# Another order for a hand-written passage, two sums on VectorE, other banks and a later sample product in the first ConvFFN slices

## The chip, the core and the metric

The kernel runs on one core of a Trainium2 chip. The core has four engines that work side by side, each through its own ordered stream of instructions: TensorE (PE) for matmuls, VectorE (DVE), ScalarE (ACT) and GpSimd (POOL) for everything elementwise. A fifth, SyncE (SP), issues most DMAs. An instruction waits at the head of its engine's stream until the semaphores it needs are set; what is queued behind it waits too. Matmul results land in PSUM banks, everything else lies in SBUF. The metric is the device time of one execution in microseconds (us); less is better.

## What is computed

One inference step of a hybrid decoder layer, for 1024 prompt rows and 64 sample rows (8 sequences of 8), with a model width of 1024. The part that matters here is the end of the attention half and the beginning of the feed-forward half:

```python
def rmsnorm(x, g):
    xf = x.astype(jnp.float32)
    y = xf * lax.rsqrt(jnp.mean(xf * xf, axis=-1, keepdims=True) + EPS)
    return (y * g.astype(jnp.float32)).astype(x.dtype)

def conv_ffn(n, prev, lw):
    a = n @ lw['ffn_w_gate']
    c = n @ lw['ffn_w_up']
    T = a.shape[1]
    full = jnp.concatenate([prev.astype(a.dtype), a], axis=1)
    w = lw['ffn_conv_w']
    conv = lw['ffn_conv_b'] + sum(w[j] * full[:, j:j + T] for j in range(CONV_W))
    y = (jax.nn.silu(conv) * c) @ lw['ffn_w_down']
    return y, full[:, full.shape[1] - (CONV_W - 1):]

def layer_forward(h, p, pos, gla_s0, conv_prev, attend, lw):
    ...
    h = h + jnp.concatenate([o_gla, o_mla], axis=-1) @ lw['w_o']
    y, conv_new = conv_ffn(rmsnorm(h, lw['g_ffn']), conv_prev, lw)
    h = h + y
```

D_FF is 2816, so `ffn_w_gate` and `ffn_w_up` are 1024 x 2816.

## The kernel before

Dense projections, the attention over the paged cache and its matmuls take the first 1310 us or so. Then the last units of the output projection run, the rows are normalised and turned into matmul operands, and ConvFFN goes over D_FF in 22 slices of 128 columns, f = 0 to 21. After them come the down-projection, the per-layer embedding and the outputs.

All matmuls are made in fp32 precision from two parts of each operand: a high part (a cast to fp32r, `high` at L1944, usually on ACT) and a low part (source minus high part, `low` at L1948 or `split` at L123 and L124). A product is three matmuls: high by high (L147), low by high (L148), high by low (L149).

A product of a slice is not made by 1024 rows times the weight. The prompt rows form tiles of 128 rows, numbered 0 to 7 (tile 8 holds the sample rows). The first six tiles and both halves of the width are combined as a fast matrix multiplication does: sums and differences of quarters of h (rows t and t + 3, halves 0 and 1 of the width; `quarter(t, i)`) are multiplied with sums and differences of weight blocks g0, g1 (gate) and u0, u1 (up). Such a product is 24 matmuls of 384 columns. The sample rows and tiles 6 and 7 are multiplied plainly in the `rest` (48 matmuls of 320 columns for gate and up). Slices 0 and 1 are not combined: they run `plain_chunk`, four `plain` products g1, g2, u1, u2 and two rests each, so that they can begin before all combinations are ready. From slice 2 on, `ff_chunk` makes the seven combined products.

The **passage** is a string PASSAGE of step names (L32 to L38) which is run inside `tc.manual_schedule` (L2098 to L2100): for PE, ACT, DVE and POOL the order of the string is the order of the streams. Its steps, with t a tile of rows and i a half of the width:

- U unit of the output projection (six matmuls, L1434, L1437, L1438), a adds it to h (DVE, L1445), q squares for the norm (ACT, L1470), s the scale: a DMA of h on ACT's queue (L1973) and the root on POOL (L1483, L1484), N normalises (DVE, L1999; for tile 6 n6 on ACT, L1996, then N6 on POOL, L1997).
- T turns a half tile (four transposes, L1939) into a PSUM bank, c casts the high part (ACT), l makes the low part (DVE, L1948), k keeps a quarter for the combinations (ACT copy L1978 for t below 3, DVE subtraction L1980 from 3 on).
- wc and wl are the two parts of slice 0's weights, vc and vl those of the last w_o pieces (casts on ACT, low parts on POOL).
- m4, lo, ptol, oL, po, oh, ol finish the sample rows' attention; d, fd, ha, hb, hq, hs, hn, HT, hc, hl are the sample rows' own chain: product with w_o (L1451, L1452), folded into `hs` (L2026, L2035, L2036), square, root, normalised row hn (DVE, L2030), two turns HT, high and low part.
- G1, X1, G2, X2 are slice 0's plain products and E its two rests.

The turns go round three PSUM banks: `(p2, p2t, p2t)[n % 3]`. X2 uses the bank of p2. The plain products of slice 0 use pd (three banks) else, the rests pm (two banks).

After the string, `sums` (L1680) makes for n = 0, 1, 2 two subtractions of quarters on POOL (L1683 into h, L1684 into `t4`) and the operands t1, t2, t3 (`put`: cast on ACT, low part on DVE). `ff_weights(f)` loads a slice's four weight blocks, casts them and makes their low parts. In a plain slice the convolution of the gate columns runs on `a` (ACT copies L1881, L1893, L1902, L1903 out of PSUM; POOL fills its edges, L1786, L1787; DVE L1776, L1778, L1906, L1908), then Silu, then the product with the up columns (L1889, L1912, L1913). The last step takes the sample rows of the result as an operand `ssm` (L1915, L1916), which `sample_rows(f, half)` multiplies with `ffn_w_down` (L1764, two matmuls a half), one slice later. `sample_weights(f, half)` loads those weights (tiles `wr`, `wdh`, `wdl`). Outside the passage a scheduler orders the streams; `issue_after` keeps an instruction behind others in its plan.

Of the kernel before, what the change touches and what calls it, by code (L numbers as in the profile page):

```python
# [18 lines left out]
P = 128  # L19
# [33 lines left out]
def step_kernel(ctx: ExitStack, tc: tile.TileContext, A):  # L53
# [68 lines left out]
    def split(hi, lo, src, lo_eng=None):  # L122
        cast = act.copy(hi, src)  # L123
        res = (lo_eng or dve).tensor_tensor(lo, src, hi.bitcast(F32), ALU.subtract)  # L124
        return cast.ins, res.ins
# [1549 lines left out]
        return hrows(t)[:, f * 512:f * 512 + 512].rearrange("p (k n) -> p k n", n=P)  # L1675

    def put(t, nm, src, eng):
        split(*(x[:, :, t * P:(t + 1) * P] for x in xb[nm]), src, eng)

    def sums(n):  # L1680

        b11, b21, t1, t2 = quarter(n, 0), quarter(n, 1), quarter(n + 3, 0), quarter(n + 3, 1)
        pool.tensor_tensor(b11, t2, b11, ALU.subtract)  # L1683
        pool.tensor_tensor(t4[n], b21.rearrange("p k n -> p (k n)"), t2.rearrange("p k n -> p (k n)"), ALU.subtract)  # L1684
# [23 lines left out]
    def ff_weights(f):  # L1708
        fs = slice(f * P, (f + 1) * P)
        raw, hl = [], wroom() if f > 1 else None  # L1710
        for nm in ("ffn_w_gate", "ffn_w_up"):
            for i in range(2):
                r = wstage()
                sp.dma_start(r, A[nm][0][i * 512:(i + 1) * 512, fs].rearrange("(k p) c -> p k c", p=P))
                raw.append(r)
        w = wgu[f] = {}
        if f < 2:
            for nm, r, eng in zip(("g0", "g1", "u0", "u1"), raw, (dve, dve, pool, pool)):
                w[nm] = block(r, eng, rooms1.pop(0))
# [24 lines left out]
    def tmp(nm):
# [14 lines left out]
    def sample_rows(f, half):  # L1759

        if f == 0:
            acc_s.append(p2t([P, 512], "ps_ds"))
        for i, w_ in enumerate(wds.pop((f, half))):
            pe.matmul(acc_s[half], chunks[f], w_, start=f == 0 and i == 0, stop=f == NF - 1 and i == 1)  # L1764

    def ff_chunk(f):
        tp = z["tp"]
# [89 lines left out]
        if not last:
            convolved()
# [17 lines left out]
    def plain_chunk(f, w, a, a_s, cv, cvs, conv, w3):  # L1876

        wgu[f] = w
        if f:
            plain(f, "g1", pd)  # L1880
        act.copy(a[:, 2:2 + NP], sums0[f, "g1"][:, :NP])  # L1881
        if not f:
            ff_weights(1)
        conv(0, NP)
        act.activation(cv[:, 0:NP], cv[:, 0:NP], AF.Silu)
        if f:
            sample_rows(late[0], 0)
            plain(f, "u1", pd)
        dve.tensor_tensor(cv[:, 0:NP], cv[:, 0:NP], sums0[f, "u1"][:, :NP], ALU.mult)  # L1889
        sample_weights(f, 0)  # L1890
        if f:
            plain(f, "g2", pd)
        act.copy(a[:, 2 + NP:2 + 2 * NP], sums0[f, "g2"][:, :NP])  # L1893
        if f:
            sample_rows(late.pop(0), 1)
            plain(f, "u2", p2)
            xb["t4"] = operand(z["xhl"], "t4", "12")
            for n in range(3):
                put(n, "t4", t4[n].rearrange("p (k n) -> p k n", n=P), dve)
            ff_weights(2)  # L1900
# [13 lines left out]
        ss_ = z["tp"].tile([P, P], F32R, tag="ssm", name="ssm", bufs=2)  # L1914
        act.copy(ss_[:, 0:R], cv[:, T:])  # L1915
        dve.tensor_tensor(ss_[:, R:2 * R], cv[:, T:], ss_[:, 0:R].bitcast(F32), ALU.subtract)  # L1916
# [48 lines left out]
    def tile_steps(t):  # L1965
# [16 lines left out]
        for i in range(2):  # L1982
            if (t, i) not in EARLY:
                later(f"U{t}{i}", lambda i=i: unit(i))
                later(f"a{t}{i}", lambda i=i: unit_sum(t, i, turns["U", t, i]))
            if (t, 1) not in EARLY:
                later(f"q{t}{i}", lambda i=i: square(t, i))
            later(f"T{t}{i}", lambda i=i: turn_of((t, i), half(t, i), P))
            later(f"c{t}{i}", lambda i=i: high((t, i, "h"), room_of(t, i), turns[t, i]))
            later(f"l{t}{i}", lambda i=i: low((t, i, "l"), room_of(t, i), turns[t, i]))  # L1990
            if t < 6:
                later(f"k{t}{i}", lambda i=i: kept(i))
        if (t, 1) not in EARLY:
            later(f"s{t}", scales)
        if t == 6:
# [498 lines left out]
```

## Time and profile before

| what | value |
|---|---|
| median of 3 runs | 2209.53 us (2209.01 to 2210.61) |
| the profiled execution, its own time | 2211.92 us |
| its span in the trace | 2210.2 us |
| mean granted PE clock | 0.984 |
| PE busy | 2133.7 us (97%), 13484 instructions |
| DVE busy | 1654.0 us (75%) |
| ACT busy | 1364.3 us (62%) |
| POOL busy | 1209.8 us (55%) |

A row of the timeline reads: start, length, engine, line, operation, output<-inputs, shape, count, and in brackets the idle time of the engine before it with the instruction that ended it. In a table of windows each row has the busy time of the engines in one stretch and then PE's granted clock. Tile numbers are left out in the trace. Matmuls are pipelined: a row's length is longer than the distance to the next one, and the distance is what a matmul costs in a row of matmuls.

### The profile page before, as it was taken

What the parts mean: (1) busy time and instruction counts of PE and PEld (TensorE: products, weight loads), DVE (VectorE), ACT (ScalarE), POOL (GpSimd) and SP (SyncE); (2) the same over time, 40 slices, a digit from 0 to 9 for tenths busy, and PEclk for the clock granted to TensorE, in tenths of its full rate; (3) what the DMA queues carried; (4) which work ended last, traced back from release to release, by engine and by line L of the source; (5) the groups of instructions that cost most, each with busy time, mean ns of one, the idle gap of its engine ahead of it and who ended that gap; (6) DMA issues with size and microseconds to landing.
All of it is one profiled execution on the core that took longest, in us unless ns stands there. A gap on an engine that the chain in (4) does not pass through costs nothing.

```text
span 2210.2 us, 38361 instructions
## 1 busy us (share of the span) xinstructions
PE 2133.7 (97%) x13484; PEld 1936.7 (88%) x13484; DVE 1654.0 (75%) x2541; ACT 1364.3 (62%) x3721; POOL 1209.8 (55%) x1316
## 2 busy tenths in 40 slices
PE   7999999999999999999999998999999999999999
PEld 6888978878888888887888878999999999888899
DVE  4685767367778888887888878788888886887642
ACT  5566766777778888887777776333333334534631
POOL 5575668576677777777455556456566562011100
PEclk9899999999999999999999999999999999999999
DMA  5343244422342222221421223232222325778321
GB/s 182 110 137 114 68 128 153 132 68 61 104 125 63 61 68 73 61 56 44 162 88 58 78 83 96 86 105 87 94 93 91 100 91 188 241 220 238 100 71 41
DMA packets 204418, 233.07 MB, mean 105 GB/s; under 512 B 42422, under 2 KB 146339, under 8 KB 204227
## 3 DMA queue, kind: packets, MB, share of 16 engines
q1 hardware_dynamic: 187971, 178.44, 25.9%
q0 software_dynamic: 15024, 47.72, 7.6%
q10 hardware_dynamic: 1232, 4.46, 0.5%
q8 instruction: 108, 1.77, 0.3%
q14 instruction: 83, 0.68, 0.1%
HBM read 188.00 MB, written 42.52 MB: 104 GB/s over the span
## 4 chain that ended last, share of the span: by engine, by line
PE 79%; DVE 7%; ACT 5%; DMA 4%; issue 2%; POOL 2%; SPq 0%; DVEq 0%; POOLq 0%; ACTq 0%
PE ps_gu L149 7%; PE ps_gu L147 7%; PE ps_gu L148 7%; PE ks L147 5%; PE ks L149 4%; PE ks L148 4%; PE ps_dn L148 3%; PE ps_dn L149 3%; PE ps_dn L147 3%; PE cpv L656 2%; PE ctp L530 2%; PE ps_lt L286 2%; PE ps_pj L147 2%; DVE css L573 2%; PE ps_pj L148 1%
## 5 line engine op out<-in xcount | busy, mean ns | idle before, releaser
L568 ACT ACTIVATE csq<-ks 128x256 f32<-128x256 f32 x1040 | 392.7, 400 | 92.7 <-PE ks L149 82.4
L573 DVE TENSOR_REDUCE css<-csq 128x16 f32<-128x1024 f32 (+1 forms) x264 | 315.7, 1196 | 59.6 <-ACT csq L568 56.7
L123 ACT CAST wh<-st 128x512 fp32r<-128x512 f32 x164 | 101.3, 619 | 174.5 <-PE ps_gu L148 165.4
L147 PE MATMUL ks<-mv0h,cTh 128*128 128x320 f32 (+1 forms) x520 | 171.3, 331 | 8.3 <-ACT sn L570 4.6
L147 PE MATMUL ks<-mv1h,cTh 128*128 128x320 f32 (+1 forms) x520 | 170.4, 329 | 7.7 <-ACT sn L570 3.5
L613 POOL TENSOR_TENSOR chl<-craw,chl 128x1024 fp32r<-128x1024 f32 x64 | 141.2, 2206 | 57.0 <-ACT chl L611 55.9
L148 PE MATMUL ks<-mv1l,cTh 128*128 128x320 f32 (+1 forms) x520 | 154.0, 298 | 0.0
L148 PE MATMUL ks<-mv0l,cTh 128*128 128x320 f32 (+1 forms) x520 | 152.5, 295 | 0.0
L149 PE MATMUL ks<-mv0h,cTl 128*128 128x320 f32 (+1 forms) x520 | 148.2, 298 | 0.9 <-DVE cTl L124 0.8
L149 PE MATMUL ks<-mv1h,cTl 128*128 128x320 f32 (+1 forms) x520 | 148.9, 300 | 0.0
L641 POOL TENSOR_TENSOR phl<-sn,phl 128x512 fp32r<-128x512 f32 (+1 forms) x63 | 84.1, 1335 | 83.7 <-ACT phl L638 83.4
L124 POOL TENSOR_TENSOR wl<-st,wh 128x512 fp32r<-128x512 f32 x42 | 65.3, 1555 | 114.7 <-ACT wh L123 114.7
L124 DVE TENSOR_TENSOR wl<-st,wh 128x512 fp32r<-128x512 f32 x122 | 108.6, 891 | 24.7 <-ACT wh L123 24.6
L149 PE MATMUL ps_dn<-o 128*128 128x512 f32 x308 | 120.2, 390 | 0.0
L148 PE MATMUL ps_dn<-o 128*128 128x512 f32 x308 | 120.1, 390 | 0.1
L124 DVE TENSOR_TENSOR cTl<-ctp,cTh 128x512 fp32r<-128x512 f32 (+1 forms) x136 | 90.0, 661 | 39.2 <-ACT cTh L123 38.3
L147 PEld LDWEIGHTS ks<-mv0h,cTh 128*128 128x128 f32 x520 | 98.3, 189 | 22.5 <-ACT sn L570 9.1
L147 PEld LDWEIGHTS ks<-mv1h,cTh 128*128 128x128 f32 x520 | 99.6, 192 | 20.0 <-ACT sn L570 7.7
L570 ACT COPY sn<-ks 128x64 f32<-128x64 f32 x520 | 116.8, 225 | 0.0
L1318 POOL TENSOR_TENSOR pl<-p,ph 128x512 fp32r<-128x512 f32 (+1 forms) x96 | 97.2, 1018 | 31.2 <-DVE ph L1317 20.7
L147 PE MATMUL ps_dn<-o 128*128 128x512 f32 x308 | 113.1, 390 | 0.0
L149 PE MATMUL ps_gu<-xrh,wl 128*128 128x320 f32 x352 | 108.8, 309 | 0.0
(705 smaller groups left out, 7872.7 us busy)
## 6 DMA issues: line engine op xcount, KB each, us to landing
raw<-ds SPq DMA_DIRECT2D x77, 256.0 KB
raw<-ffn_w_down SPq DMA_DIRECT2D x66, 256.0 KB
stage<-w_in SPq DMA_DIRECT2D x48, 256.0 KB
wr<-ffn_w_down SPq DMA_DIRECT2D x44, 256.0 KB
st<-ffn_w_gate SPq DMA_DIRECT2D x42, 256.0 KB
st<-ffn_w_up SPq DMA_DIRECT2D x42, 256.0 KB
ds<-cv SPq DMA_DIRECT2D x19, 512.0 KB
oraw<-doT SPq DMA_DIRECT2D x16, 256.0 KB
```

What stands on the lines that cost most here:

```text
L123: cast = act.copy(hi, src)
L124: res = (lo_eng or dve).tensor_tensor(lo, src, hi.bitcast(F32), ALU.subtract)
L147: pe.matmul(ps, ah, bh, start=first, stop=False)
L148: pe.matmul(ps, ah, bl, start=False, stop=False)
L149: return pe.matmul(ps, al, bh, start=False, stop=last)
L286: pe.matmul(ps, x, w, start=first, stop=last)
L568: act.activation(sq[:, f * 256:f * 256 + 256], ks[:, 0:256], AF.Square)
L570: act.copy(o.sn[:, g0 + i, :], ks[:, 256:320])
L573: dve.tensor_reduce(o.ss[:, g0 + i + 1 - n:g0 + i + 1, :].rearrange("p i h -> p (i h)"), sq2[:, :n].rearrange("p i (h n) -> p (i h) n", n= ...
L613: pool.tensor_tensor(ch[:, c0:c1, 128:256], src, ch[:, c0:c1, 0:128].bitcast(F32), ALU.subtract)
L641: (dve if drain == 2 else pool).tensor_tensor(phl[:, :nt, 64:128], sb, phl[:, :nt, 0:64].bitcast(F32), ALU.subtract)
L1318: pool.tensor_tensor(pl[:, c0:], p[:, c0:], ph[:, c0:].bitcast(F32), ALU.subtract)
```

## The change

Five things are edited.

1. The PASSAGE string has another order, and it has three new steps b0, b1, b2: the POOL subtraction `quarter(t, 0) = quarter(t + 3, 1) - quarter(t, 0)`, which `sums` made after the string before.
2. The three t4 subtractions are made by DVE, behind the operands t1 to t3.
3. Slice 1's weights: all four low parts are made by DVE (u0 and u1 were POOL's), and `ff_weights(1)` is issued with `sums`.
4. Slice 1's products: g1 and g2 go to banks of p2t, u1 and u2 to pd, in the order g1, g2, u1, u2; g1 is issued after E.
5. The sample product of slice 0 is made in slice 2 and no longer in slice 1; that of slice 1 stays in slice 2, near its end. Slices 1 and 2 load their `ffn_w_down` pieces in slice 2. From slice 3 on all is as before.

```diff
 PASSAGE = (
-    "wc0 wc1 N0 U41 wc3 T01 a41 wc2 k01 c01 N1 U50 l01 T11 T10 vc1 U51 c11 a50 T00 wl3 c10 N2 k11 k10 a51 vl1 U71 "
-    "l10 U70 wl1 l11 T21 q51 a71 k00 lo q40 m4 T20 N3 ptol U61 wl0 a70 q41 c00 c21 c20 s4 oL U60 po q50 vc2 l00 k21 "
-    "s5 l21 l20 N4 oh1 vc3 k20 N5 a60 T30 a61 q71 c30 k30 T31 oh0 vl2 l30 vl3 G1 c31 wl2 T50 vc0 q61 T40 ol1 q70 "
-    "q60 ol0 c50 vl0 s7 d1 l31 k31 T51 fd1 k50 k40 X1 c40 l50 T41 s6 n6 ha1 d0 N7 k51 c51 c41 hb1 N6 l51 l40 l41 "
-    "T71 hq1 fd0 k41 ha0 T61 c71 c61 T70 hb0 G2 l71 c70 l70 hq0 hs T60 l61 hn0 c60 HT0 hn1 HT1 X2 hc0 hl0 hc1 hl1 "
-    "l60 E ")
+    "N0 wc0 wc3 wc2 wl0 U70 a70 wc1 q70 U71 U60 vc0 N2 N1 T20 T00 a71 U61 vl0 a60 c20 T21 c00 a61 k20 l00 vc1 l20 "
+    "c21 q71 wl3 T11 wl2 N3 U41 k21 lo m4 c11 s7 U50 k11 U51 l11 k00 vl1 T30 l21 ptol q40 a50 wl1 T01 vc2 vl2 c30 "
+    "oL a41 c01 k30 T10 c10 l30 q41 po l01 oh0 l10 N7 vc3 a51 oh1 k01 T31 q50 G1 k31 s4 k10 ol0 vl3 ol1 c31 N4 q51 "
+    "l31 d1 T40 T41 s5 q61 N5 k40 d0 q60 c40 c41 l40 T50 fd1 ha1 T51 s6 hb1 l41 n6 c50 X1 k41 fd0 N6 k50 c51 hq1 "
+    "l50 T60 T61 b1 l51 k51 T70 c60 G2 c61 ha0 hb0 b2 l60 c70 l70 l61 hq0 T71 hs c71 hn1 hn0 l71 HT1 HT0 hc0 hl0 "
+    "hc1 b0 hl1 X2 E ")
...
-        b11, b21, t1, t2 = quarter(n, 0), quarter(n, 1), quarter(n + 3, 0), quarter(n + 3, 1)
-        pool.tensor_tensor(b11, t2, b11, ALU.subtract)
-        pool.tensor_tensor(t4[n], b21.rearrange("p k n -> p (k n)"), t2.rearrange("p k n -> p (k n)"), ALU.subtract)
+        b11, t1, t2 = quarter(n, 0), quarter(n + 3, 0), quarter(n + 3, 1)
...
-            for nm, r, eng in zip(("g0", "g1", "u0", "u1"), raw, (dve, dve, pool, pool)):
-                w[nm] = block(r, eng, rooms1.pop(0))
+            for nm, r in zip(("g0", "g1", "u0", "u1"), raw):
+                w[nm] = block(r, dve, rooms1.pop(0))
...
+    def both_rows(f):
+
+        for half in range(2):
+            sample_rows(f, half)
+        late.pop(0)
...
         m6 = product("s2", "t2")
         dve.tensor_tensor(v, m6, v, ALU.add)
-        if late:
+        if f == 2:
+            both_rows(0)
+            for half in range(2):
+                sample_weights(1, half)
+        else:
             sample_rows(late[0], 0)
-        sample_weights(f, 0)
+            sample_weights(f, 0)
...
         if not last:
             pu = up_rest()
+        if f == 2:
+            both_rows(1)
+            for half in range(2):
+                sample_weights(2, half)
...
         if f:
-            plain(f, "g1", pd)
+            with tc.issue_after(v["E"]):
+                plain(f, "g1", p2t)
+            plain(f, "g2", p2t)
         act.copy(a[:, 2:2 + NP], sums0[f, "g1"][:, :NP])
-        if not f:
-            ff_weights(1)
         conv(0, NP)
         act.activation(cv[:, 0:NP], cv[:, 0:NP], AF.Silu)
         if f:
-            sample_rows(late[0], 0)
             plain(f, "u1", pd)
         dve.tensor_tensor(cv[:, 0:NP], cv[:, 0:NP], sums0[f, "u1"][:, :NP], ALU.mult)
-        sample_weights(f, 0)
-        if f:
-            plain(f, "g2", pd)
+        if not f:
+            sample_weights(f, 0)
         act.copy(a[:, 2 + NP:2 + 2 * NP], sums0[f, "g2"][:, :NP])
         if f:
-            sample_rows(late.pop(0), 1)
-            plain(f, "u2", p2)
+            plain(f, "u2", pd)
...
+        if t < 3:
+            later(f"b{t}", lambda: pool.tensor_tensor(quarter(t, 0), quarter(t + 3, 1), quarter(t, 0), ALU.subtract))
...
-    with tc.issue_after(v["hc", 1]), tc.issue_after(v["hl", 1]), tc.issue_after(v["hs"]):
+    with tc.issue_after(v["hc", 1]), tc.issue_after(v["hl", 1]), tc.issue_after(v[6, 0, "l"]):
+        ff_weights(1)
         for n in range(3):
             sums(n)
+    with tc.issue_after(z["put"][1]):
+        for n in range(3):
+            dve.tensor_tensor(t4[n].rearrange("p (k n) -> p k n", n=P), quarter(n, 1), quarter(n + 3, 1), ALU.subtract)
```

The streams are the same up to the passage and, but for a few neighbours, from slice 3 on. Three places show what moves.

PE's stream at the beginning of the passage, before. The rows with `ps_dn` are the units U, those with `pt` the turns of h (tile names h_14701, h_14702, h_14703 are the tiles 0, 1, 2):

```order
6630 L1939 MATMUL pt<-ident,h_14701 128x128 x4
6631 L1434 MATMUL ps_dn<-wdh,sh 128x512
...
6636 L1438 MATMUL ps_dn<-wdh,sl 128x512
6637 L1939 MATMUL pt<-ident,h_14702 128x128 x8
6638 L1434 MATMUL ps_dn<-wdh,sh 128x512
```

And of the change, some rows further on, where its first turns stand:

```order
6641 L1438 MATMUL ps_dn<-wdh,sl 128x512
6642 L1950 MATMUL pt<-ident,h_14703 128x128 x4
6643 L1950 MATMUL pt<-ident,h_14701 128x128 x4
6644 L1434 MATMUL ps_dn<-wdh,sh 128x512
...
6649 L1438 MATMUL ps_dn<-wdh,sl 128x512
6650 L1950 MATMUL pt<-ident,h_14703 128x128 x4
6651 L1950 MATMUL pt<-ident,h_14702 128x128 x4
```

The turns begin one unit later than before, with tile 2 in place of tile 0, and T11 is the fourth turn (T20, T00, T21, T11), so in the round of three banks it gets that of T20.

DVE's stream behind the sample rows' norm, before; `xt1l` to `xt3l` are the low parts of t1 to t3, and h_14698 to h_14700 the tiles 3 to 5:

```order
1576 L2030 SCALAR_TENSOR_TENSOR hn<-hs,rs,gb 64x512 x2
1577 L124 TENSOR_TENSOR wl<-st,wh 128x512 x2
1578 L1948 TENSOR_TENSOR xrl<-pt,xrh 128x4x64 x2
1579 L1948 TENSOR_TENSOR xrl<-pt,xrh 128x4x128
1580 L124 TENSOR_TENSOR xt1l<-h_14698,xt1h 128x4x128
...
1588 L124 TENSOR_TENSOR xt3l<-h_14703,xt3h 128x4x128
1589 L1776 TENSOR_SCALAR cv<-a,convT 128x384
```

The same place with the change; L2130 is the t4 subtraction:

```order
1574 L2043 SCALAR_TENSOR_TENSOR hn<-hs,rs,gb 64x512 x2
1575 L1959 TENSOR_TENSOR xrl<-pt,xrh 128x4x128
1576 L1959 TENSOR_TENSOR xrl<-pt,xrh 128x4x64 x2
1577 L124 TENSOR_TENSOR wl<-st,wh 128x512 x4
1578 L124 TENSOR_TENSOR xt1l<-h_14698,xt1h 128x4x128
...
1586 L124 TENSOR_TENSOR xt3l<-h_14703,xt3h 128x4x128
1587 L2130 TENSOR_TENSOR wh<-h_14701,h_14698 128x512
1588 L2130 TENSOR_TENSOR wl<-h_14702,h_14699 128x512
1589 L2130 TENSOR_TENSOR wh<-h_14703,h_14700 128x512
1590 L124 TENSOR_TENSOR wl<-st,wh 128x512 x3
1591 L1780 TENSOR_SCALAR cv<-a,convT 128x384
```

The sample rows' low parts now stand ahead of the weights' low parts, and between them and the first operation of the convolution stand 19 operations where 9 stood. On POOL, five operations leave this place: the three of L1684 and the two low parts; two of the sums go ahead of the sample rows' root:

```order
880 L2005 TENSOR_TENSOR h_14702<-h_14699,h_14702 128x512
881 L2005 TENSOR_TENSOR h_14703<-h_14700,h_14703 128x512
882 L1483 TENSOR_SCALAR ss<-ss 64x1
883 L1484 TENSOR_TENSOR rs<-ss,mhalf 64x1
884 L2005 TENSOR_TENSOR h_14701<-h_14698,h_14701 128x512
885 L1723 TENSOR_TENSOR st<-st 128x512
886 L1724 TENSOR_TENSOR st<-st 128x512
887 L1790 MEMSET a 128x2
```

The third sum stands right behind the root, and the sums of slice 2's weights (L1723, L1724) right before the fill of `a`.

PE's stream inside slice 1, before; `x21` and `x12` are operands of the plain products:

```order
6888 L148 MATMUL ps_gu<-x21l,wh 128x384
6889 L1764 MATMUL ps_ds<-wdh,ssm 128x512
6890 L1764 MATMUL ps_ds<-wdl,ssm 128x512
6891 L149 MATMUL ps_gu<-x21h,wl 128x384
6892 L147 MATMUL ps_gu<-x12h,wh 128x384
```

The same place with the change:

```order
6888 L148 MATMUL ps_gu<-x22l,wh 128x384
6889 L149 MATMUL ps_gu<-x22h,wl 128x384
6890 L147 MATMUL ps_gu<-x11h,wh 128x384
6891 L148 MATMUL ps_gu<-x11l,wh 128x384
6892 L149 MATMUL ps_gu<-x11h,wl 128x384
```

The sample matmuls have left slice 1 (their first is row 7022 now, in slice 2), and g2 (operands x12, x22) is made ahead of u1 (operands x11, x21).

More of the change, by code (lines that the diff above doesn't have):

```diff
@@ L1677, in put @@
     def put(t, nm, src, eng):
-        split(*(x[:, :, t * P:(t + 1) * P] for x in xb[nm]), src, eng)
+        z["put"] = split(*(x[:, :, t * P:(t + 1) * P] for x in xb[nm]), src, eng)
     def sums(n):
-        b11, b21, t1, t2 = quarter(n, 0), quarter(n, 1), quarter(n + 3, 0), quarter(n + 3, 1)
-        pool.tensor_tensor(b11, t2, b11, ALU.subtract)
-        pool.tensor_tensor(t4[n], b21.rearrange("p k n -> p (k n)"), t2.rearrange("p k n -> p (k n)"), ALU.subtract)
+        b11, t1, t2 = quarter(n, 0), quarter(n + 3, 0), quarter(n + 3, 1)
         put(n, "t1", t1, dve)
@@ L1739, in rest @@
             for k in range(4):
-                mm3(ps[:, :NR], w[nm][0][:, k], w[nm][1][:, k], xr[0][:, 4 * i + k], xr[1][:, 4 * i + k],
-                    i == k == 0, i == 1 and k == 3)
+                z["rest"] = mm3(ps[:, :NR], w[nm][0][:, k], w[nm][1][:, k], xr[0][:, 4 * i + k], xr[1][:, 4 * i + k],
+                    i == k == 0, i == 1 and k == 3).ins
         return ps
@@ L1847, in ff_chunk @@
         pool.tensor_tensor(m5c, m5c, v, ALU.add)
-        if late:
-            sample_rows(late.pop(0), 1)
-        if not last:
-            sample_weights(f, 1)
+        if 2 < f:
+            if late:
+                sample_rows(late.pop(0), 1)
+            if not last:
+                sample_weights(f, 1)
         m4 = product("u1", "t4")
@@ L1886, in plain_chunk @@
         if f:
-            sample_rows(late[0], 0)
             plain(f, "u1", pd)
         dve.tensor_tensor(cv[:, 0:NP], cv[:, 0:NP], sums0[f, "u1"][:, :NP], ALU.mult)
-        sample_weights(f, 0)
-        if f:
-            plain(f, "g2", pd)
+        if not f:
+            sample_weights(f, 0)
         act.copy(a[:, 2 + NP:2 + 2 * NP], sums0[f, "g2"][:, :NP])
         if f:
-            sample_rows(late.pop(0), 1)
-            plain(f, "u2", p2)
+            plain(f, "u2", pd)
             xb["t4"] = operand(z["xhl"], "t4", "12")
@@ L1916, in plain_chunk @@
         dve.tensor_tensor(ss_[:, R:2 * R], cv[:, T:], ss_[:, 0:R].bitcast(F32), ALU.subtract)
-        sample_weights(f, 1)
+        if not f:
+            sample_weights(f, 1)
         pool.dma_start(ds[f], cv[:, 0:T])
@@ L2098, in step_kernel @@
     assert not steps, steps
+    v["E"] = z["rest"]
     for nm in ("sg", "wf"):
```

## The prediction

> **What bounds the kernel now.** I read the table of windows first, around the end of the hand-written string, then PE's timeline there, since PE is busy 97% of the span and only its idle or slow time can be won.
>
> ```profile
> core 0: us, PE busy (x) PEld busy (x) DVE busy (x) ACT busy (x) POOL busy (x), PEclk, DMA share, GB/s
> 1360.00:1380.00 20.00, 15.71 (x90) 15.39 (x91) 13.54 (x20) 10.19 (x20) 16.89 (x13) 0.83 0.26 69
> 1380.00:1400.00 20.00, 16.38 (x78) 15.78 (x77) 13.29 (x22) 6.35 (x14) 4.88 (x7) 0.83 0.29 93
> 1420.00:1500.00 80.00, 80.00 (x482) 79.38 (x481) 69.25 (x92) 31.62 (x63) 48.73 (x48) 1.00 0.30 96
> ```
>
> Two things are to be seen: from 1360 to 1400 PE idles and its granted clock is 0.83, and from 1420 it is full (80.00 of 80). So what is won before slice 2 is carried to the end unchanged, and nothing can be won behind it. PE's timeline says where the idle time lies:
>
> ```profile
> 1322.97 0.39 PE L1434 MATMUL ps_dn<-wdh,sh 128*128 128x512 f32 x1
> 1324.36 0.60 PE L1939 MATMUL pt<-ident,h 128*128 128x128 f32 x4
> 1324.71 0.48 PE L1434 MATMUL ps_dn<-wdh,sh 128*128 128x512 f32 x1
> ...
> 1346.94 0.42 PE L147 MATMUL ps_gu<-x11h,wh 128*128 128x384 f32 x1
> ...
> 1351.20 0.60 PE L1939 MATMUL pt<-ident,h 128*128 128x128 f32 x4
> ...
> 1362.09 1.32 PE L1939 MATMUL pt<-ident,hn 64*128 64x64 f32 x8 [2.51 <-DVE hn L2030]
> 1365.61 0.69 PE L147 MATMUL ps_gu<-x12h,wh 128*128 128x384 f32 x1 [2.20 <-DVE xrl L1948]
> ...
> 1371.36 0.31 PE L147 MATMUL ps_gu<-xrh,wh 128*128 128x320 f32 x1
> ...
> 1378.39 0.34 PE L147 MATMUL ps_gu<-x11h,wh 128*128 128x384 f32 x1
> ...
> 1390.35 0.80 PE L1764 MATMUL ps_ds<-wdh,ssm 128*128 128x512 f32 x1 [3.62 <-DVE ssm L1916]
> 1390.95 0.63 PE L1764 MATMUL ps_ds<-wdl,ssm 128*128 128x512 f32 x1
> ...
> 1396.17 0.35 PE L149 MATMUL ps_gu<-x22h,wl 128*128 128x384 f32 x1
> ...
> 1409.60 0.34 PE L147 MATMUL ps_gu<-x21h,wh 128*128 128x384 f32 x1
> ```
>
> Two waits carry it. X2 (1365.61) waits for the sample rows' chain, and slice 1 stands 3.62 us for `ssm`, the end of slice 0's convolution. After both, matmuls run at half clock. From start to start the rows give the units I use: a unit U 1.39 (1322.97 to 1324.36), a turn T 0.35, a plain product 4.26 (1346.94 to 1351.20), a sample product d, eight matmuls of a unit's kind, 8 x 1.39 / 6 = 1.86, the two rests 7.03 (1371.36 to 1378.39).
>
> **The change, term 1: the `ssm` wait (products of two slices in slice 2, other banks).** The wait of 3.62 goes. Its slow stretch goes too: from 1390.35 to 1396.17, 5.82 us, PE issues 17 matmuls, two of the sample and 15 plain ones; at full clock these are 2 x 0.23 and 15 x 0.173 (24 take 4.26, less the slower first), 3.07, so 2.75 were lost. The four sample matmuls themselves (0.94) only move to slice 2. Slice 1, 31.21 us now, becomes 23.9, and its last wait is another one. What is late next is `ps_gu` of its rests: they need the bank that slice 0's convolution frees, and that hangs on DVE and POOL:
>
> ```profile
> 1366.08 0.67 DVE L124 TENSOR_TENSOR xt1l<-h,xt1h 128x512 fp32r<-128x512 f32 x1
> ...
> 1370.89 0.67 DVE L124 TENSOR_TENSOR xt3l<-h,xt3h 128x512 fp32r<-128x512 f32 x1
> 1377.95 0.53 DVE L1776 TENSOR_SCALAR cv<-a,convT 128x384 f32<-128x384 f32 x1 [6.38 <-POOL a L1786]
> 1365.99 6.74 POOL L1684 TENSOR_TENSOR wh<-h,h 128x512 f32<-128x512 f32 x1
> 1372.69 2.55 POOL L124 TENSOR_TENSOR wl<-st,wh 128x512 fp32r<-128x512 f32 x2
> ```
>
> L1684's last subtraction takes 6.74 on POOL, against 1.28 for one of the pair below it, exactly while DVE runs nine low parts at 0.60 apart (1366.08 to 1370.89): DVE's run of operations with two inputs in SBUF locks POOL out until it ends. The changed DVE runs 18 of these in a row (four low parts of weights, nine of rows, three t4, two weights), 18 x 0.60 = 10.8 from about 1364.5 to 1375.4. POOL's L1723 and L1724 for slice 2 are shut out as long. But POOL has lost the three t4 and two weight parts ahead of the `a` fill, so the convolution starts about where it does now, 1379 for 1377.95. Today its end, `ssm`, lets PE go at 1390.35, just after the last product has read the bank; so the bank comes free at some 1389 to 1391. Slice 1's last rest needs it at the end of the first four products and the first rest, 16.7 + 3.5 = 20.2 after slice 1's start, about 1397. Slack 6 to 8 us: cost nothing. If the cover goes, each further us costs one us.
>
> [...]
>
> In slice 2 the eight sample matmuls wait for `ssm` of slice 0 (about 1391) and of slice 1. The first come some 6 us behind slice 2's start (near 1407), the second 20 us behind, 13 us later than slice 1's own `ssm`. Nothing there stalls by my reckoning. The two extra low parts of w_down on DVE, 1.2 us, lie in a stage with 80 - 69.25 = 10.75 free.
>
> **Term 2: the new string, up to X2.** Both start at 1322.97 with the same work, so only waits differ. My walk: U70, U71, U60 (3 x 1.39) to 1327.14; T20, T00, U61, T21 to 1329.6. T11 takes the bank of T20, so it waits for l20, which DVE now has behind a61 and l00:
>
> ```profile
> 1329.01 0.69 DVE L1445 TENSOR_TENSOR h<-h,ps_dn 128x512 f32<-128x512 f32 x1
> 1329.62 0.69 DVE L1948 TENSOR_TENSOR x11l<-pt,x11h 128x512 fp32r<-128x512 f32 x1
> ```
>
> These follow 0.61 apart; three behind U61's end (1329.45) give 1331.3. **PE idles about 1.85** where it idles nothing now. Bounds: 0, were l20 ahead of a61, and 3.5, were three more operations ahead of l20 late as well (3 x 0.61). Then T11, U41, U50, U51, T30, ptol, T01, T10, po, T31 to 1338.8; G1 waits for l10, 0.7 (bounds 0 and 2, one more lock of a POOL operation); G1 ends near 1343.8. d1, T40, T41, d0, T50, T51, X1 follow without a wait to 1353.25. T60 then waits for tile 6's scale:
>
> ```profile
> 1346.95 0.33 ACTq L1973 DMA_DIRECT2D dhp<-h  x1
> 1349.66 1.15 ACT L1996 ACTIVATE h<-h,rs 128x1024 f32<-128x1024 f32 x1 [1.68 <-DMA dhp<-h]
> 1350.89 2.40 POOL L1997 TENSOR_TENSOR h<-h,gb 128x1024 f32<-128x1024 f32 x1 [4.80 <-ACT h L1996]
> 1357.65 3.74 POOL L1683 TENSOR_TENSOR h<-h,h 128x512 f32<-128x512 f32 x3
> 1357.72 4.89 DVE L2030 SCALAR_TENSOR_TENSOR hn<-hs,rs,gb 64x512 f32<-64x512 f32 x2
> ```
>
> The DMA goes out at 1348.05 by my walk along ACT, lands 2.71 later (1346.95 to 1349.66), 1.15 and 2.40 follow: 1354.4, **PE idle 1.25** (0 to 2.5). T60, T61, T70 and G2 then end at 1359.85, well ahead of X2.
>
> X2 does not wait for PE's lateness but for the sample chain, and there the three row sums matter. Today hn starts with L1683's three (3.74) and needs 4.89 for the pair, so about 3.7 is the lock. With two of the sums ahead of the chain, only b0 (3.74 / 3 = 1.25) stands beside hn. But ha0 now falls behind b1 and b2 (to 1356.85), hb0, the square and the root end at 1359.9, b0 to 1361.15, hn1 and hn0 at 0.6 each ((4.89 - 3.74) / 2) to 1362.35, two turns, the cast and hl0 to **1364.15**. X2 so starts 1365.61 - 1364.15 = 1.46 earlier. Bounds of X2: 1362.5 (no lock from b1, b2 and b0) to 1366.5 (both locks, and N6 2.5 late). T11's and G1's waits mostly vanish in the wait for this chain; at their upper ends T's and d0 come late enough to pass 1 us on.
>
> From X2 on, nothing changes (5.75 to the rests, 7.03 for these), and I keep the slow clock of today in it: 5.75 where a product takes 4.26, 1.5 lost.
>
> **Moves costed at nothing.** Weight casts and low parts of slice 0 and w_o come earlier in the string than their users; slice 1's weights on DVE are done by 1375.4, before slice 1 at about 1377; its u products come at about 1385.5. The t4 sums on DVE are used only in slice 2. SP's loads keep their place.
>
> **Sum.** 3.62 + 2.75 + 1.46 = 7.83 against the profiled run: its span 2210.2, its own time 2211.92, would be 2204.09. The median of the runs shown is 2209.53, so **2201.7**. A measurement of this kernel can tell about 0.2%, 4.4 us, from no change.
>
> **The clock, weighed.** Slow stretches follow short waits, 2.51 above and 1.78 here:
>
> ```profile
> 1071.56 0.39 PE L147 MATMUL ks<-mv0h,cTh 128*128 128x256 f32 x1 [1.78 <-ACT sn L570]
> 1072.38 0.47 PE L148 MATMUL ks<-mv0l,cTh 128*128 128x320 f32 x1
> ```
>
> After 1.78 idle, a 320-column matmul takes 0.47 (0.31 at full clock, the row at 1371.36). The new string's waits, T11's 1.85 and the two of about 1.5 around HT, stand at this edge. [...] Without it the 1.5 within X2 goes too, and the sum would be 9.3, 2200.2.
>
> **Rivals.**
> 1. *Forecast*, gain 6 to 9.3: 2200.2 to 2203.5. Chance 0.49.
> 2. *Clock stays full and the new locks hide.* X2 at 1362.6 and no slow stretch: 7.83 + 1.55 + 1.5 = 10.9, 2198.7. For it: waits at the edge, PSUM inputs that need no lock. Against: b0 goes ahead of hn on POOL. 0.20.
> 3. *The new waits at T11 and N6 slow the clock.* One stretch like today's is 6.8 us at half clock, up to 3.4 lost, two with the later turns more: gain 2 to 5, 2204.5 to 2207.5, about 2206. For it: 1.85 is above 1.78. Against: PE has some 2 to 3 us in hand before X2. 0.16, half of it faster by the bound below.
> 4. *The sample wait only moves.* The eight matmuls of slice 2 wait for `ssm` or w_down instead, 3.6 and 2.7 come back: gain 1.5, 2208.0. Against: the 13 us above. 0.08.
> 5. *Slower.* DVE's run shuts POOL out; slice 2's weights (L1723, L1724) come late, ACT has their casts ahead of its copies into `a`, and slice 0's convolution, which frees the last bank of slice 1, slips. It costs from 7 us late on; with 2.7 of slow clock it eats the gain at 7 + 7.8 - 2.7 = 12.1 late. A slip of 20, about two locked runs of 10.8, gives 20 - 7 + 2.7 - 7.8 = 7.9 slower: 2217.4. For it: 6.74 against 1.28. Against: POOL has five operations fewer. 0.05.
> 6. *It does nothing*: X2 no earlier, another wait in slice 1 for `ssm`'s: 2209.5. 0.02.
>
> Faster by over 0.2%: 0.49 + 0.20 + 0.08 = 0.77. Within: 0.08 + 0.08 + 0.02 = 0.18. Slower: 0.05. The range 2197.5 to 2207.5 leaves out rivals 4, 5, 6 and a little of the ends of 2 and 3.
>
> **What would show it.** Right: no wait for `ssm` in slice 1 and full clock in it, slice 2 starting 7.83 + 0.94 earlier, near 1400.8 for 1409.60; a wait of T11 on `x11l` or its neighbour near 2, one of T60 on N6 near 1.2, hn's pair near 2.5 for 4.89. Wrong: an idle PE in slice 1 released by slice 0's `cv`, a POOL L1723 of over 15 us, or sample matmuls in slice 2 with a wait.

## The result, and the profile after

The changed kernel takes 2198.52 us (median of 5 runs, 2197.84 to 2201.36) against 2209.53 us before: 11.0 us less, a ratio of 0.9953 with a 95% interval of 0.9939 to 0.9968. The forecast was 2201.7, 7.8 us less, with a range of 2197.5 to 2207.5. So the sign and the range held. The gain came out 3.2 us larger: the time lies outside the forecast's own 2200.2 to 2203.5 and within 0.2 us of rival 2 (2198.7).

The table of windows of the changed kernel shows the region that was to be won (columns as before, the clock is the last number but two):

```profile
1360.00:1380.00 20.00, 19.98 (x122) 19.98 (x123) 16.75 (x27) 12.16 (x24) 12.15 (x10) 1.00 0.22 67
1380.00:1400.00 20.00, 20.00 (x125) 20.00 (x124) 16.93 (x28) 9.72 (x19) 8.52 (x12) 1.00 0.29 92
```

PE is full from 1360 on, 19.98 and 20.00 of 20 for 15.71 and 16.38, and its clock is 1.00 for 0.83. PE's timeline gives the marks: the first unit of the passage, the wait of T11, X2, the first rest, slice 1, slice 2.

```profile
1320.38 0.39 PE L1434 MATMUL ps_dn<-wdh,sh 128*128 128x512 f32 x1
...
1329.07 0.63 PE L1950 MATMUL pt<-ident,h 128*128 128x128 f32 x4 [1.63 <-DVE x11l L1959]
...
1360.02 0.44 PE L147 MATMUL ps_gu<-x12h,wh 128*128 128x384 f32 x1 [0.92 <-DVE xrl L1959]
...
1364.29 0.31 PE L147 MATMUL ps_gu<-xrh,wh 128*128 128x320 f32 x1
...
1371.33 0.34 PE L147 MATMUL ps_gu<-x11h,wh 128*128 128x384 f32 x1
...
1395.03 0.34 PE L147 MATMUL ps_gu<-x21h,wh 128*128 128x384 f32 x1
```

Counted from the first unit, where the streams of both kernels part, the marks divide the gain:

| stretch | before | after | won | forecast |
|---|---|---|---|---|
| first unit to X2 | 42.64 | 39.64 | 3.00 | 1.46 |
| X2 to the rests | 5.75 | 4.27 | 1.48 | 0 |
| the rests | 7.03 | 7.04 | 0 | 0 |
| slice 1, less the 0.94 that move | 30.27 | 23.70 | 6.57 | 6.37 |
| sum | | | 11.05 | 7.83 |

The sum agrees with the difference of the medians, 11.01, more closely than their interval (7 to 13.5 us less) could promise. The two profiled executions differ by more, 2211.92 - 2198.30 = 13.62, because this one reaches the first unit 2.59 us earlier (1320.38 for 1322.97), where both kernels have the same streams; that part is none of the change's.

DVE and POOL around the sample rows' chain, in the changed kernel (L2005 are the row sums b, L2048 is ha0, L2043 hn):

```profile
1351.68 2.98 POOL L2005 TENSOR_TENSOR h<-h,h 128x512 f32<-128x512 f32 x2
1356.04 1.28 POOL L2005 TENSOR_TENSOR h<-h,h 128x512 f32<-128x512 f32 x1
1365.22 7.20 POOL L1723 TENSOR_TENSOR st<-st 128x512 f32<-128x512 f32 x1 [7.90 <-DMA st<-ffn_w_up]
...
1352.32 1.19 DVE L2048 TENSOR_TENSOR hs<-hs,fd 64x512 f32<-64x512 f32 x1
1356.10 2.43 DVE L2043 SCALAR_TENSOR_TENSOR hn<-hs,rs,gb 64x512 f32<-64x512 f32 x2
1369.98 1.29 DVE L124 TENSOR_TENSOR wl<-st,wh 128x512 fp32r<-128x512 f32 x2
```

hn's pair takes 2.43 for 4.89, since only one row sum stands beside it. ha0 took 1.19, half of it waiting (ha1, the same operation, took 0.68): it went between b1 and b2, and did not wait for both. POOL's L1723 was shut out from 1365.22 until DVE's run ended at 1371.27; it took 7.20, L1724 behind it 1.29.

### The profile page after: what moved, and what is told of

It is laid out like the page before. It is cut to its first block, busy times and chain, and to the rows that moved or that the text cites. A ratio compares the mean times of both kernels' runs of the same rounds, so it can differ in the third digit from the quotient of the medians.

```text
span 2196.6 us, 38367 instructions
## 1 busy us (share of the span) xinstructions
PE 2125.2 (97%) x13484; PEld 1929.4 (88%) x13484; DVE 1654.9 (75%) x2546; ACT 1363.5 (62%) x3721; POOL 1207.0 (55%) x1311
## 3 DMA queue, kind: packets, MB, share of 16 engines
q8 instruction: 108, 1.77, 0.3%
## 4 chain that ended last, share of the span: by engine, by line
PE 81%; DVE 8%; ACT 5%; DMA 3%; issue 1%; POOL 1%; SPq 0%; DVEq 0%; ACTq 0%; POOLq 0%
PE ps_gu L147 7%; PE ps_gu L148 7%; PE ps_gu L149 7%; PE ks L147 5%; PE ks L149 4%; PE ks L148 4%; PE ps_dn L148 3%; PE ps_dn L149 3%; PE ps_dn L147 3%; PE cpv L656 2%; PE ctp L530 2%; PE ps_lt L286 2%; DVE css L573 2%; PE ps_pj L147 2%; PE ps_pj L148 1%
```

## The experiments

Each kernel is read by the same marks. Each ratio is to runs of the kernel before on the same chip (medians 2209.22 and 2209.39 beside the kernels of the experiments). A dash in the last column marks a kernel of which one time was taken.

| kernel | first unit to X2 | X2 to rests | first unit to slice 2 | median us | ratio to before, 95% |
|---|---|---|---|---|---|
| before | 42.64 | 5.75 | 86.63 | 2209.53 | 1 |
| the change | 39.64 | 4.27 | 74.65 | 2198.52 | 0.9953, 0.9939 to 0.9968 |
| the change again | 39.67 | 4.27 | 74.67 | 2198.73 | 0.9947, 0.9934 to 0.9961 |
| edits 4 and 5 alone | 42.62 | 7.10 | 80.46 | 2203.46 | 0.9967, 0.9953 to 0.9981 |
| edits 1 to 3 alone | 39.63 | 5.85 | 79.23 | 2202.21 | 0.9972, 0.9961 to 0.9983 |
| edit 5 undone | 39.64 | 4.27 | 76.25 | 2198.39 | 0.9950, 0.9934 to 0.9966 |
| t4, u0, u1 on POOL | 42.13 | 5.84 | 78.70 | 2204.18 | 0.9970, 0.9959 to 0.9981 |
| row sums behind the root | 41.70 | 5.86 | 78.29 | 2201.75 | - |
| the same, hn in two operations | 42.62 | 6.95 | 80.30 | 2201.93 | - |
| row sums ahead of the root | 39.51 | 4.29 | 74.53 | 2200.88 | - |
| l20, l00 and b0 earlier | 38.63 | 4.30 | 73.66 | 2200.71 | 0.9955, 0.9942 to 0.9968 |

Where the sample product of slice 0 stands in slice 1 (before, edits 1 to 3 alone, edit 5 undone), 0.94 us of the fourth column is that work.

### Edits 4 and 5 alone

```diff
         if f:
-            plain(f, "g1", pd)
+            with tc.issue_after(v["E"]):
+                plain(f, "g1", p2t)
+            plain(f, "g2", p2t)
...
-            sample_rows(late[0], 0)
             plain(f, "u1", pd)
...
+        if f == 2:
+            both_rows(0)
```

> Before with the fourth and fifth edit alone: slice 1's products in other banks and order, slice 0's sample product in slice 2; the old passage, sums and weight parts stay. Theory A (terms add up): the ssm wait of 3.62 us and its slow stretch of 2.75 us go, X2 still waits for the sample rows' chain and its slow clock stays, so X2 starts 42.6 us behind the passage's first unit as before, and the time falls by 6.4 us, ratio near 0.997. Theory B (the old sums on POOL make the next wait): the convolution of slice 0 frees the last bank of slice 1 too late, PE waits in slice 1 for cv or ps_gu, and the gain is under 4 us.

Slice 1 takes 23.70, as in the whole change: theory A holds for the wait. The old passage keeps its waits, and X2 still runs slow:

```profile
1359.53 1.32 PE L1954 MATMUL pt<-ident,hn 64*128 64x64 f32 x8 [2.51 <-DVE hn L2045]
1363.04 0.69 PE L147 MATMUL ps_gu<-x12h,wh 128*128 128x384 f32 x1 [2.19 <-DVE xrl L1963]
1370.14 0.31 PE L147 MATMUL ps_gu<-xrh,wh 128*128 128x320 f32 x1
```

X2 lasts 7.10 here (1363.04 to 1370.14) for 5.75 in the profile of before: the slow stretch reached over nearly all of it. That is why the gain is 86.63 - 0.94 - 80.46 = 5.2 and not 6.4.

### Edits 1 to 3 alone

```diff
 PASSAGE = (
-    "wc0 wc1 N0 U41 ...
+    "N0 wc0 wc3 wc2 ...
...
-        pool.tensor_tensor(t4[n], b21.rearrange("p k n -> p (k n)"), t2.rearrange("p k n -> p (k n)"), ALU.subtract)
+    with tc.issue_after(z["put"][1]):
+        for n in range(3):
+            dve.tensor_tensor(t4[n].rearrange("p (k n) -> p k n", n=P), quarter(n, 1), quarter(n + 3, 1), ALU.subtract)
```

> Before with the first three edits alone: the new passage, the row sums in it, t4 and all of slice 1's weight low parts on VectorE; the sample product of slice 0 stays in slice 1. Theory A (terms add up): X2 starts 39.6 us behind the first unit instead of 42.6 and runs at full clock, a gain of 4.5 us, and the wait for ssm in slice 1 stays near 3.6 us with its slow stretch. Theory B (the scheduler, whose order follows the new passage, puts the sample matmuls some 36 matmuls later): the wait shrinks to 0 to 2 us without a slow clock, and the gain is 8 to 11 us, nearly all of the change. Theory C: slice 0's convolution comes later relative to slice 1's start, the wait grows to 6 us and the gain is under 2 us.

For the wait theory B holds: there is none for `ssm` in slice 1, although the sample product is still made there. The scheduler has put its matmuls 83 matmuls behind slice 1's start, where 47 stood between them before, and the products stand in their old order (g1, u1, g2, u2). The full clock in X2 and the gain of 8 to 11 us did not come: the marks show 7.4 (86.63 - 79.23). One reason is a wait that no theory had:

```profile
1359.10 0.61 PE L147 MATMUL ps_gu<-x12h,wh 128*128 128x384 f32 x1 [0.92 <-DVE xrl L1944]
1360.15 0.52 PE L147 MATMUL ps_gu<-x12h,wh 128*128 128x384 f32 x1
1361.11 0.52 PE L147 MATMUL ps_gu<-x12h,wh 128*128 128x384 f32 x1
...
1364.96 0.31 PE L147 MATMUL ps_gu<-xrh,wh 128*128 128x320 f32 x1
...
1373.92 0.45 PE L147 MATMUL ps_gu<-x11h,wh 128*128 128x384 f32 x1 [1.77 <-ACT a L1879]
...
1373.40 0.47 ACT L1879 COPY a<-ps_gu 128x384 f32<-128x384 f32 x1
...
1364.25 7.24 POOL L1723 TENSOR_TENSOR st<-st 128x512 f32<-128x512 f32 x1 [7.86 <-DMA st<-ffn_w_up]
```

Slice 1's first product waits 1.77 us for the bank that ACT's copy into `a` frees at 1373.87. That copy stands behind casts which wait for POOL, and POOL's L1723 was shut out for 7.24 by DVE's run. So the run that edits 2 and 3 lengthen has its price, and edit 4 avoids it by taking g1 into a bank of p2t. X2 stands behind the same waits as in the changed kernel (0.23 and 0.92), and yet ran at half clock: its matmuls are 0.32 apart from 1360.15 to 1361.11, three for 0.96, where they are 0.17 apart at full clock in the changed kernel. That is 1.58 us (5.85 for 4.27) without a difference in the work.

The two halves, 5.2 and 7.4 us by the marks, add to 12.6 and not to 11.05. Each removes the `ssm` wait by itself, so the 6.4 to 6.6 of slice 1 are counted twice. Against that, X2 is 1.35 slower than before with edits 4 and 5, and with edits 1 to 3 it does not win its 1.48, and slice 1 begins 1.94 late.

### Edit 5 undone

```diff
         if f:
+            sample_rows(late[0], 0)
             plain(f, "u1", pd)
```

> The changed kernel with its fifth edit undone: slice 0's sample product is again made in slice 1, with all else as in the change. Theory A (what removes the ssm wait is that the product goes to slice 2): the wait comes back with 3 us or more and a slow stretch behind it, and the kernel is 4 to 6 us slower than the changed one. Theory B (the new order of the products, with the sample matmuls 84 matmuls behind slice 1's start instead of 48, is enough): a wait under 1 us, no slow stretch, and a time within 1.5 us of the changed kernel's.

```profile
1383.38 0.50 PE L1762 MATMUL ps_ds<-wdh,ssm 128*128 128x512 f32 x1 [0.40 <-DVE ssm L1918]
```

Theory B: a wait of 0.40, no slow stretch, and a time of 2198.39 against 2198.73 on the same chip. With edits 1 to 4 in place the sample product could have stayed in slice 1, where its matmuls stand 84 behind the start; what it costs there is 76.25 - 0.94 - 74.67 = 0.6 us by the marks.

### t4 and the low parts u0, u1 on POOL again

```diff
+        pool.tensor_tensor(t4[n], b21.rearrange("p k n -> p (k n)"), t2.rearrange("p k n -> p (k n)"), ALU.subtract)
...
-            for nm, r in zip(("g0", "g1", "u0", "u1"), raw):
-                w[nm] = block(r, dve, rooms1.pop(0))
+            for nm, r, eng in zip(("g0", "g1", "u0", "u1"), raw, (dve, dve, pool, pool)):
+                w[nm] = block(r, eng, rooms1.pop(0))
```

> The changed kernel with the t4 subtractions and the low parts u0 and u1 of slice 1's weights on POOL again. POOL's fill of a comes some 4 to 5 us later. Theory A (slice 0's convolution has 5.6 us of slack before slice 1's last rest, 1385.9 against 1391.5, and the copies into a have about 5 us before u1 takes their bank): PE waits under 0.5 us in slice 1, and the time is within 1 us of the changed kernel's; the move to VectorE gained nothing by itself. Theory B: the slack is used up, PE waits 1 to 4 us in slice 1 on ACT's copies into a or on cv, and the time rises by 1 to 5 us.

Both theories looked in the wrong place. Slice 1 has no wait (23.70, the slack holds), and still the median rises by 5.45 us (2204.18 for 2198.73; by the marks 4.03, and what the rest is remains open). POOL's fill of `a` did not come 4 to 5 us later either, but 1.7 earlier (51.6 us behind the first unit for 53.3); POOL and DVE took turns there, at 1.74 to 1.77 an operation. The loss is ahead of X2:

```profile
1355.37 1.29 POOL L2006 TENSOR_TENSOR h<-h,h 128x512 f32<-128x512 f32 x1
1356.62 2.48 POOL L1683 TENSOR_TENSOR wh<-h,h 128x512 f32<-128x512 f32 x2
...
1355.43 4.88 DVE L2044 SCALAR_TENSOR_TENSOR hn<-hs,rs,gb 64x512 f32<-64x512 f32 x2
...
1359.80 0.43 PE L1951 MATMUL pt<-ident,hn 64*128 64x64 f32 x4 [2.55 <-DVE hn L2044]
```

Two t4 subtractions now follow b0 on POOL without a pause, and hn's first operation waits for all three, until 1359.10. X2 comes 2.49 later, and is slow again for a part (5.84 for 4.27). So the move of t4 to DVE is worth 2.5 us and, where X2 then takes 4.27, some 4, not for the time it takes from POOL, but because it ends POOL's run behind the root. In the prediction it was costed at nothing.

### Row sums all behind the root, and all ahead of it

```diff
-    "hc1 b0 hl1 X2 E ")
+    "hc1 b0 b1 b2 hl1 X2 E ")
```

> The changed kernel with b1 and b2 moved behind b0, so that POOL makes its three row sums behind the sample rows' root, as before the change. Theory A (a run of POOL's operations holds hn until its end): hn's pair takes 4.9 us instead of 2.4, X2 starts some 1.3 us later than in the changed kernel (2.5 of hn less the 0.6 to 1.2 that ha0 wins), 40.9 us behind the first unit, and PE idles about 2.2 us before X2 in two pieces. [...] Theory B (VectorE gets in between two of POOL's operations): hn's pair stays at 2.4 us and X2 starts 0.6 us earlier than in the changed kernel.

```diff
-    "l50 T60 T61 b1 l51 k51 T70 ...
+    "l50 T60 T61 b0 b1 l51 k51 T70 ...
```

> The changed kernel with b0 moved ahead of b1, so that POOL makes its three row sums in one run ahead of the sample rows' root. Theory A (VectorE gets in behind the operation that runs): ha0 takes at most 1.3 us as now (1.19), hn's pair falls from 2.4 to 1.3 us, X2 starts about 0.6 to 1.2 us earlier, 38.4 to 39.0 us behind the first unit. Theory B (a run of POOL's operations holds VectorE until its end): ha0 takes 3 us or more, the root comes 1.5 to 2.5 us later and eats what hn wins; X2 starts 39.6 to 41 us behind the first unit.

Each diff shows where the moved sums arrive; they leave their old places in the string. First the three sums and hn of the kernel that has them behind the root, then the three sums, ha0 and hn of the one that has them ahead:

```profile
1355.47 3.74 POOL L2005 TENSOR_TENSOR h<-h,h 128x512 f32<-128x512 f32 x3
1355.53 4.88 DVE L2043 SCALAR_TENSOR_TENSOR hn<-hs,rs,gb 64x512 f32<-64x512 f32 x2 [0.20 <-POOL rs L1484]
```

```profile
1354.39 4.23 POOL L2005 TENSOR_TENSOR h<-h,h 128x512 f32<-128x512 f32 x3
1355.01 1.20 DVE L2048 TENSOR_TENSOR hs<-hs,fd 64x512 f32<-64x512 f32 x1
1359.67 1.41 DVE L2043 SCALAR_TENSOR_TENSOR hn<-hs,rs,gb 64x512 f32<-64x512 f32 x2 [0.95 <-POOL rs L1484]
```

Behind the root, theory A: hn waits for the whole run, 4.88 for the pair, X2 is 2.06 later (41.70; 1.3 was expected) and slow. Ahead of it, theory A as well: ha0 takes 1.20 and starts after one of three sums. Its X2 however comes only 0.13 earlier, not 0.6 to 1.2: POOL's longer run (4.23) delays the root, and eats what hn wins.

### hn in two operations

This starts from the kernel that has the three sums behind the root.

```diff
-            dve.scalar_tensor_tensor(v["hn", f], hs, z["rs"][:R, NT:NT + 1], z["gb"][:R, f * 512:f * 512 + 512],
-                                     ALU.mult, ALU.mult)
+            dve.tensor_scalar(v["hn", f], hs, z["rs"][:R, NT:NT + 1], None, ALU.mult)
+            dve.tensor_tensor(v["hn", f], v["hn", f], z["gb"][:R, f * 512:f * 512 + 512], ALU.mult)
```

> The kernel with all three row sums behind the root, with hn made by two operations of VectorE, a tensor_scalar by rs and then a tensor_tensor by gb, in place of one scalar_tensor_tensor. Everywhere else in the traces VectorE gets its turn behind the POOL operation that runs (ha0 waits 0.6 us and starts between two row sums); hn alone waited 4.2 us for the whole run of three. Theory A (it is hn's form, an operation whose scalar POOL has just written): the tensor_tensor starts behind b0, 1.3 us after the root, hn is done 2.5 us earlier than with one operation, and X2 starts 39.6 to 40.2 us behind the first unit. Theory B (it is the place: an operation that arrives while a run of POOL has just begun waits for its end): the tensor_scalar or the tensor_tensor is held until the third sum ends, as hn was, and X2 starts at 41.5 us or later.

```profile
1353.68 3.73 POOL L2005 TENSOR_TENSOR h<-h,h 128x512 f32<-128x512 f32 x3
1353.74 3.95 DVE L2043 TENSOR_SCALAR hn<-hs,rs 64x512 f32<-64x512 f32 x1 [0.19 <-POOL rs L1484]
1357.72 0.68 DVE L2044 TENSOR_TENSOR hn<-hn,gb 64x512 f32<-64x512 f32 x1
```

Theory B: even the plain scaling, with one tensor as input, waits for the end of POOL's run (3.95, where its second takes 0.47). So it is not the form of hn with three inputs.

### The change again, and l20, l00 and b0 earlier

> The changed kernel once more, beside the next ones on the same chip. All theories: the stretch from the passage's first unit to slice 2 takes 74.6 us as before, if X2 runs at full clock, and some 76.2 us if a half-clock stretch of 3.4 us falls into X2, as it did in the kernel with the first three edits alone behind the same waits; so runs should lie in two groups some 1.6 us apart, at about 2198 and 2200 us.

The stretch repeats to 0.02 us (74.67). The runs, from 2197.41 to 2200.56, do not fall into two groups, so that expectation failed; what is ahead of the passage varies by as much (the two profiles of the change reach the first unit at 1320.38 and 1321.57).

```diff
-    "N0 wc0 ... U61 vl0 a60 c20 T21 c00 a61 k20 l00 vc1 l20 "
+    "N0 wc0 ... U61 vl0 a60 c20 l20 T21 c00 l00 a61 k20 vc1 "
...
-    ... s6 hb1 l41 n6 c50 X1 ... hc1 b0 hl1 X2 E ")
+    ... s6 hb1 l41 n6 b0 c50 X1 ... hc1 hl1 X2 E ")
```

> The changed kernel with two moves in the string: l20 and l00 ahead of a61 on VectorE, so that T11 need not wait for U61 and its sum, and b0 ahead of N6 on POOL, where POOL idles 4 us. Theory A (T11's wait of 1.63 us is PE time that counts, and b0's lock of hn 1.2 us): T11 waits under 0.3 us, hn's pair takes 1.4 us, X2 starts 1.2 to 1.7 us earlier, 38.0 to 38.4 us behind the first unit instead of 39.64, and the time falls by as much, ratio to the changed kernel 0.9993. Theory B (the chain over the scale of tile 5 and 6, their DMAs and N6 sets the time of T60 and of ha0, not PE): T11's wait goes and comes back at T40, T60 or X2, and X2 starts within 0.4 us of 39.5.

```profile
1336.04 1.06 PE L1950 MATMUL pt<-ident,h 128*128 128x128 f32 x8 [0.54 <-DVE x21l L1959]
...
1361.50 0.45 PE L147 MATMUL ps_gu<-x12h,wh 128*128 128x384 f32 x1 [1.09 <-DVE xrl L1959]
```

T11 no longer waits, hn's pair takes 1.40, and X2 comes 1.01 us earlier (38.63); a third of T11's wait comes back as 0.54 at a later turn. This lies between the theories, nearer to A. The median, 2200.71 (2198.0 to 2202.05), does not show it: it is 2.0 us above that of the change again, and the two intervals overlap for the most part. Whether this version is faster stays open.

## Why the prediction came out as it did

**The `ssm` wait (6.37 forecast, 6.57 measured).** Size right: slice 1 is at full clock and without a wait. The reason given is only half of it. "Products of two slices in slice 2" was named as what removes the wait, and with edit 5 undone the wait is 0.40. What does it there is that the sample matmuls stand 84 matmuls behind slice 1's start and not 47. Edits 1 to 3 alone bring them to 83 with the products in their old order, so the new order is not needed for it: the scheduler's plan behind the new string pushes them back. Which of the three edits moves the plan was not tried. The other banks, named in the same breath, are needed for something else, the 1.77 us for g1's bank: edits 1 to 4 together do not have that wait.

**The new passage (1.46 forecast, 3.00 measured).** The turns begin two units later than in the old string (rows 6642 and 6630 of PE's stream), as the walk along PE has it, and not one unit later, as the section on the change says. That walk was close: T11 idles 1.63 (1.85 forecast), G1's two waits sum to 0.55 (0.7), N6 ends 31.3 us behind the first unit (31.4). T60's wait of 1.25 did not appear, since X1 ended a good us later than walked and met N6. The step that was mis-sized reads "ha0 now falls behind b1 and b2 (to 1356.85)". It fell behind b1 alone: it ended 33.1 us behind the first unit, not 34.5 (b2's end by the walk, 33.9, and 0.6 of its own), and these 1.35 us are nearly all of the 1.54 that X2 came earlier. The case of hn and the three sums had been taken as the rule for a run of POOL; ha0 shows that it isn't always.

**The slow clock in X2 (kept at 1.5, gone).** The prediction's 9.3 and 2200.2 are its sum with these 1.5 us won as well. Here rival 2 was the better reading. Its X2 fits as well (1362.6, or 39.63 behind the first unit, for 39.64), but in part by luck: it had the locks of POOL hidden, and b0 did hold hn, 2.43 for the pair where 1.40 is what it takes alone; the time was won at ha0. The waits around HT and X2 sum to 1.15 us in the changed kernel, and 4.7 before. In the profiles, X2 was slow in all five kernels with 3 us or more of such waits, and in one of six with 1.09 to 1.15 us, that of edits 1 to 3 alone. Both profiles of the change itself show full clock, but the slow one stood behind the same waits, so the 1.48 us need not come in every execution.

**The lock of POOL behind X2.** DVE's run lasted 10.9 us (1360.34 to 1371.27; 10.8 forecast). L1723 was not shut out for all of it, since its own DMA let it start only at 1365.22; it took 7.20, as the 6.74 row suggested. The convolution began 55.5 us behind the first unit, against 55.0 before, and kept its slack in slice 1. The mechanism of rival 5 is real, though: without edit 4 it cost 1.77 us, at g1's bank and not at the last rest, where it was looked for.

**Moves costed at nothing.** The t4 sums were among them. They were priced by what waits for their result; their place was in the way of another engine, and that was worth 2.5 us, or 4 with the clock.

**The other rivals** (the sample wait only moves, new waits slow the clock) did not occur; slice 2 starts without a wait.

## What to carry to other kernels

Price an operation that leaves an engine not only by its users, but by what it held up on another engine: here the last operation of a run on POOL set when hn could begin on VectorE, 4.88 us for its pair behind three operations and 2.43 behind one. Where a wait is removed in two ways at once, undo each alone; their gains overlap, and one of the edits may only be along for the ride. A wait of PE has a second price in its clock, and it is paid behind some waits and not behind others of the same length (behind 1.15 us of them X2 took 5.85 in one kernel and 4.27 in another), so a gain of a us or two is read from the marks of a stretch before it is read from medians.

## What the runs showed of the hardware

VectorE and POOL did not share in one way. The first hn operation waited for the end of a run of three POOL operations, 4.2 us, in the kernel before and in three others with such a run behind the root, and so did a plain scaling by one tensor. ha0 got its turn after one POOL operation (1.19 and 1.20), with another queued behind it. L1723 on POOL waited for some ten VectorE operations (7.2). With t4 on POOL the two took turns, one operation each, as these rows of that kernel show:

```profile
1365.04 1.77 DVE L124 TENSOR_TENSOR xt2l<-h,xt2h 128x512 fp32r<-128x512 f32 x1
...
1366.21 1.75 POOL L1683 TENSOR_TENSOR wl<-h,h 128x512 f32<-128x512 f32 x1
1367.93 1.74 POOL L1724 TENSOR_TENSOR st<-st 128x512 f32<-128x512 f32 x1
```

A turn after one operation (ha0 and these rows) and a wait for a whole run (hn 4.2, L1723 7.2) so stand side by side. The scaling by one tensor waited like hn: 3.95, where its second operation took 0.47 and the product of the same shape 0.68. Operations of VectorE with an input in PSUM were not held: in the kernel before, three low parts out of pt (from 1351.32) took 0.68 to 0.69 each while POOL's N6 ran (2.40 from 1350.89), and in the changed kernel the 64 sums with `ps_dn` took 0.67 to 0.69, also those beside a POOL operation. What decides between a turn and a whole run stays open: the operation's form was tried and is not it. In the rows shown of these kernels, hn and the scaling arrive 0.06 us behind the start of the run's first operation and ha0 some 0.6 behind that of one; whether that decides was not tried.

The clock fell behind short waits: 1.15 us in all ahead of X2 in the kernel with edits 1 to 3 alone. T11's single wait of 1.63 did not slow it in any profile; in the changed kernel the granted clock is 1.00 from 1294.3 on. The same waits gave full clock in one kernel and half clock in another, so the length of a wait alone does not decide.

The traces bear on what else might. Within one trace the granted clock changes only at steps of 3.41 us (24 changes in the kernel before, 18 in the changed one), and the slow stretches around X2 and `ssm` last one, two or three of them; in the kernel before they last 6.84 and 6.82 us, at a granted clock of 0.50. Two such steps of the kernel with edits 1 to 3 alone, then two of the changed kernel at the same place:

```profile
1355.80:1359.21 3.41, 2.16 (x18) 1.68 (x16) 3.08 (x5) 1.58 (x4) 0.60 (x1) 1.00 0.08 23
1359.22:1362.63 3.41, 3.41 (x11) 3.41 (x12) 3.38 (x7) 3.41 (x8) 0.00 (x0) 0.50 0.49 149
```

```profile
1355.76:1359.17 3.41, 3.02 (x22) 2.53 (x21) 3.28 (x4) 0.62 (x2) 1.56 (x2) 1.00 0.27 56
1359.18:1362.59 3.41, 2.57 (x15) 2.57 (x16) 3.09 (x7) 3.41 (x8) 0.00 (x0) 1.00 0.31 90
```

In the first kernel both waits fall into one step, PE idles 1.25 us of it (3.41 - 2.16), and the next step has half clock. In the changed kernel the end of a step divides them, 0.39 and 0.84 idle, and the clock stays full. The other four kernels with these waits have 0.87 to 1.09 idle in their fullest step there, and full clock. So the place of the waits in the steps fits as what decided in X2; no run moved it on purpose. Idle time in a step has no sharp edge, though. In the kernel before, steps with 1.54 and 1.62 us idle (from 655.46 and 1027.51) were followed by half clock, and one with 1.60 (from 447.25) by full clock. In the kernel with the sums behind the root a step with 1.88 idle (from 1356.21) was followed by full clock, and the next, with 1.42, by half.
